# Gaps of 64 bytes between tiles: where moving and stationary operands begin in a partition

## The chip, the cores and the metric

The kernel runs on one core of a Trainium2 chip. The metric is the device time of one execution in microseconds (us). TensorE (PE in the profile) multiplies, VectorE (DVE), ScalarE (ACT) and GpSimd (POOL) do elementwise work, SyncE (SP) issues most of the DMA transfers. On-chip memory (SBUF) has 128 partitions; a tile takes the same range of bytes in each of them.

## What is computed

Two transformer blocks in a row on 256 tokens of width 1024, all in float32. The first block: convolution mixers, attention to a memory of 256 rows, and a PEER layer, which scores all 16,384 experts densely here. The second: two kinds of attention and an MLP. Cut to the parts that fill the time:

```python
def conv_mixers(h, w_in, ...):
    proj = jnp.einsum('bsd,dc->bsc', h, w_in)              # 1024 -> 7168
    ...                                                    
def peer_ffn(h, w_pq, subkeys, u, v):
    q = jnp.einsum('bsd,dq->bsq', h, w_pq)
    ... # 16 best of 128 x 128 experts per token and head: indices and gates
    act = gelu(einsum('chkd,cd->chk', u[idx], h)) * gates
    return einsum('chk,chkd->cd', act, v[idx])             # 16384 experts of width 1024
def second_block(x, ...):
    ...
    y = jnp.square(jax.nn.relu(h2 @ w_up)) @ w_down        # 1024 -> 4096 -> 1024
```

## The kernel before, in words

**Units.** Every weight matrix is cut into units of 128 output columns by 1024 rows (512 KB); there are 493 of them. SyncE loads a unit into a tile `w` (L332), ScalarE rounds it to a high part `wh` (L298), GpSimd, or VectorE in some stages, subtracts that to get a low part `wl` (L302). Each of `w`, `wh`, `wl` has three buffers of 4096 bytes per partition. The activations are kept as a high and a low part too. A product is then high x high, high weight x low activation and low weight x high activation: 24 matmuls of 128 x 128 by 128 x 256 per unit, the 16 with `wh` first, then the 8 with `wl`. Each matmul has its own weight load, and the profile shows the load of the next one under the matmul that runs.

**Stationary and moving.** In `blk` (L380) and `acc_unit` (L1421, L1423, L1425) the unit is stationary and an activation tile moves. In `go_v` (L815 to L819) it is the other way round: `memHL` is stationary and the unit moves. The moving tiles, in the order of the program: `e0a`/`e0b` (L380, first units), `hN` (most of the input projection), `memHL`, `eA`/`eB`, `mg`, `q`, `oA`/`oB`, `p`, then `hA`/`hB` for the 128 units of the experts' first matrix, `zz` for the 128 units of their second, the `s` tiles (second block), `oaHL`/`obHL`, `m`, `eu0`/`eu1` for the 32 units of w_up and `uHL` for the 32 of w_down.

**Stages around the experts.** During units 0 to 47 of the first matrix VectorE finds the best 16 keys and candidates. Then it builds the gates in batches of 8 tokens (L1294, L1298, L1301), which TensorE turns into gate matrices with small matmuls (L1313) that are put between units; the gates of the second group of experts are made during units 48 to 75 and just behind them, those of the first group during units 76 to 127 and the beginning of the second matrix. In the second matrix VectorE also makes the low part of `zz` (L248), one per unit, two units ahead.

**Order.** A planner (`Sched`) with a cost for each operation sets the order when the program is built; each engine then runs its instructions in that order.

**Where tiles lie.** Pools are opened one behind the other, and tiles follow each other in the order of their first use in a pool, each rounded up to 32 bytes. Stages that follow each other take over the same space.

Of the kernel before, what the change touches and what calls it, by code (L numbers as in the profile page):

```python
# [19 lines left out]
F32 = mybir.dt.float32  # L20
# [163 lines left out]
def c_dve(n, ap=0, fast=False):  # L184
    return 66 + n / (1.92 if fast else 0.96) + 60 * ap
# [15 lines left out]
def c_pool(n):  # L201
    return 150 + 2.1 * n
# [8 lines left out]
def tile_kernel(ctx, tc, A, out):  # L211
# [4 lines left out]

    cpool = ctx.enter_context(tc.tile_pool(name="const", bufs=1))
    wpool = ctx.enter_context(tc.tile_pool(name="w", bufs=3))
    epool = ctx.enter_context(tc.tile_pool(name="e", bufs=1))
    mm = ctx.enter_context(tc.tile_pool(name="mm", bufs=4, space=PSUM))  # L220
    ms = ctx.enter_context(tc.tile_pool(name="ms", bufs=4, space=PSUM))
# [28 lines left out]
    def act(o, a, f, **kw):  # L250
        return lambda e="act": ACT.activation(o, a, f, **kw)  # L251

    def either(n):
        return (("dve", c_dve(n), 0.0), ("pool", c_pool(n), 0.0))

    vec = cpool.tile([128, NV], F32, name="vec")
    cst = cpool.tile([128, NCONST], F32, name="cst")
    epsc = cpool.tile([128, 2], F32, name="epsc")
# [4 lines left out]
    def vcol(name, j=0, w=1):  # L263
        return vec[:, VC[name] + j:VC[name] + j + w]
# [170 lines left out]
    def tokens(o, accs, first=True):  # L435

        for t in range(2):
            for i, a in enumerate(accs):
                PE.matmul(o[:, t:t + 1], a[:, t * 128:(t + 1) * 128], onesD[:, 0:1],
                          start=first and t == 0 and i == 0, stop=i == len(accs) - 1, skip_group_check=True)  # L440

    def spread(R, st, bank, ev, n=2, dg=None, copy=()):

        if dg is None:
            dg = cpool.tile([128, n, 128], F32, tag="dg", bufs=1, name="dg")

        def f():
            b = bank()
            for i in range(n):
                PE.matmul(b[:, i * 128:(i + 1) * 128], onesD, dg[:, i], start=i == 0, stop=True, skip_group_check=True)  # L450

        yield Op("dve", 80.0, lambda: V.reciprocal(st, st))
        yield Op("dve", c_dve(n * 128), lambda: V.tensor_tensor(
            dg, ident[:, None, :].to_broadcast([128, n, 128]), st[:, :, None].to_broadcast([128, n, 128]), op=OP.mult))
        yield Op("pe", 215.0 * n, f, ev=(ev, "p"))
        if copy is not None:
            yield Op("act", c_act(n * 128), lambda: ACT.activation(R, bank()[:, :n * 128], AF.Copy), deps=copy, ev=ev)
# [40 lines left out]
    P1 = p1.enter_context(tc.tile_pool(name="p1", bufs=1))  # L498
# [102 lines left out]


    glu = P1.tile([128, 8, 30 + S], F32, name="glu")
    cc = P1.tile([128, 8, S], F32, name="cc")
    POOL.memset(glu[:, :, 0:30], 0.0)
    cfa = {}
# [172 lines left out]
        yield Op("dve", c_dve(S), tt(cfHL[:, 1, j], cc[:, j], cfHL[:, 0, j].bitcast(F32), OP.subtract), ev=("cf", j))  # L779


    kHL = P1.tile([128, 2, 8, S], FR, name="kHL")
    vHL = P1.tile([128, 2, 2, D], FR, name="vHL")

# [737 lines left out]
    P3 = p3.enter_context(tc.tile_pool(name="p3", bufs=1))  # L1522
# [6 lines left out]
    aS2 = P3.tile([128, 2, S], F32, tag="CQ", name="aS2")  # L1529
    RRA = P3.tile([128, 2 * S], F32, name="RRA")  # L1530
    RR, RA = RRA[:, 0:S], RRA[:, S:2 * S]

    def x1_tile(n):
        yield Op("dve", c_dve(S), tt(x1[:, n], xr[:, n], vacc[n // 2][:, (n % 2) * S:(n % 2 + 1) * S], OP.add),
                 ev=("x1", n))
        yield from hl_gain(e02[0][:, n], e02[1][:, n], x1[:, n], g12[:, n:n + 1], S, None, ("xi", n))
# [14 lines left out]

    def x1_stats():
        b = vacc[0][:, 256:260]
        st = P3.tile([128, 4], F32, name="st4")

        def f():
            tokens(b[:, 0:2], [aS1[:, 0], aS1[:, 1]])
            tokens(b[:, 2:4], [aS2[:, 0], aS2[:, 1]], first=False)

        yield Op("pe", 1000.0, f, deps=[("aS", 0, 3), ("aS", 1, 3)])  # L1560

        yield Op("dve", 130.0, lambda: V.tensor_scalar(st[:, 2:4], b[:, 0:2], EPS, None, op0=OP.add))
        yield Op("dve", 130.0, lambda: V.scalar_tensor_tensor(
            st[:, 0:2], st[:, 2:4], EPS, b[:, 2:4], op0=OP.mult, op1=OP.add))
        yield Op("act", 190.0, act(st, st, AF.Sqrt, scale=1.0 / D ** 2))
        dg = T3.tile([128, 2, S], F32, tag="sg", bufs=3, name="sg").rearrange("p a (b t) -> p (a b) t", b=2)
        yield from spread(RRA, st, lambda: vacc[1], "RR", n=4, dg=dg)
        for n in range(8):
            yield Op("dve", c_dve(S, 1), lambda n=n: V.scalar_tensor_tensor(
                xn[:, n], x1[:, n], vcol("final_g", n), RA, op0=OP.mult, op1=OP.mult), ev=("xn", n))  # L1570

    sch.spawn(x1_squares(0), prio=200.0, ready=sch.vt["pe"])
    sch.spawn(x1_squares(1), prio=200.0, ready=sch.vt["pe"])
    sch.spawn(x1_stats(), prio=0.0, ready=sch.vt["pe"])
    acc_last(u_V[128 - NLAST:], vacc, [zs(n) for n in range(128 - NLAST, 128)],
             [("zz", n) for n in range(128 - NLAST, 128)],
# [4 lines left out]
    P3a = p3a.enter_context(tc.tile_pool(name="p3a", bufs=1))  # L1581
# [13 lines left out]
    ckHL = cqk[:, 4:6]  # L1595
    krM = P3a.tile([128, 2, 4, S], FR, name="krM")
    kaM = P3a.tile([128, 2, 2, S], FR, name="kaM")
    vaP = P3a.tile([128, 2, 2, 128], FR, name="vaP")
    vbP = P3a.tile([128, 2, 2, 512], FR, name="vbP")
    qaHL = P3a.tile([128, 2, 4, S], FR, name="qaHL")  # L1600
    qnHL = P3a.tile([128, 2, 4, S], FR, name="qnHL")
    qrHL = P3a.tile([128, 2, 2, S], FR, name="qrHL")
    accq = T3.tile([128, S], F32, tag="acc2", bufs=1, name="accq")
    RQK = P3.tile([128, 2, S], F32, tag="Rq", name="RQK")
    Rq, Rk = RQK[:, 0], RQK[:, 1]
# [585 lines left out]
```

## Time and profile before

| | us |
|---|---|
| median of 3 runs | 1763.25 |
| lowest and highest | 1757.76 and 1767.33 |
| profiled execution, its own time | 1760.9 |
| its span, first to last instruction | 1759.1 |

| engine | busy us | share | instructions |
|---|---|---|---|
| PE | 1587.0 | 90% | 12948 |
| DVE | 1336.5 | 76% | 2197 |
| POOL | 1140.9 | 65% | 486 |
| ACT | 848.8 | 48% | 1463 |

Mean granted TensorE clock: 0.949 of full speed (2.4 GHz); at the lower level it is 0.5 (1.2 GHz).

Matmuls are pipelined: each is shown with some 0.28 us, and the next begins long before it ends. The time of a stream of matmuls is therefore read from their starts. A row of the view in order of time that stands for the 8 matmuls with `wl` comes once per unit, so the distance of two such starts is the time of 24 matmuls. The chain of waits follows the execution back from its last instruction to whatever released each step; its shares say on which engine and line the end depended in a stretch.

### The profile page before, as it was taken

The page shows a single profiled execution, that of the slowest core. Times are in us where ns is not written, and L with a number is a line of the kernel's source. Part 1 is how long each engine was busy: PE and PEld are TensorE (multiplying, and loading weights), DVE is VectorE, ACT ScalarE, POOL GpSimd, SP SyncE. Part 2 cuts the span into 40 slices and gives each one's busy share as a digit, 9 for nine tenths or more (in the row PEclk, how much of TensorE's full clock was granted, in tenths as well). Part 3 has the DMA queues.
Part 4 walks back from the last instruction along what each step waited for, and adds up shares of the span by engine and source line. Part 5 has one row for each costly group of instructions (what it writes and reads, how often), then busy time and mean ns, then how long its engine had stood idle before and what let it go on. Part 6 is the DMA issues. An engine that isn't in the chain of part 4 may idle for free.

```text
span 1759.1 us, 32653 instructions
## 1 busy us (share of the span) xinstructions
PE 1587.0 (90%) x12948; PEld 1562.7 (89%) x12948; DVE 1336.5 (76%) x2197; ACT 848.8 (48%) x1463; POOL 1140.9 (65%) x486
## 2 busy tenths in 40 slices
PE   8899989899999598388997889999999889979997
PEld 7899989889999598278897889999999779979997
DVE  7889967659895778998888998898987896464302
ACT  5544455554445344244444344445455465556533
POOL 6788756456788401057675668888887534758885
PEclk8999989999999799589998999999999899989999
DMA  5565545344555354034443445555555322535553
GB/s 194 169 199 196 168 144 168 120 148 148 165 182 177 103 173 145 1 120 138 139 145 120 143 133 181 187 187 180 182 186 172 121 83 78 179 121 187 181 186 113
DMA packets 75305, 266.69 MB, mean 152 GB/s; under 512 B 8721, under 2 KB 9233, under 8 KB 75153
## 3 DMA queue, kind: packets, MB, share of 16 engines
q1 hardware_dynamic: 73856, 262.77, 45.8%
q8 instruction: 101, 1.65, 0.4%
q10 hardware_dynamic: 1296, 1.85, 0.3%
q14 instruction: 52, 0.42, 0.1%
HBM read 262.48 MB, written 2.10 MB: 150 GB/s over the span
## 4 chain that ended last, share of the span: by engine, by line
PE 65%; DVE 27%; issue 3%; ACT 3%; DMA 1%; POOL 1%; SPq 0%; DVEq 0%; ACTq 0%; POOLq 0%
PE mmb L380 35%; PE msb L1423 8%; PE msb L1425 8%; PE msb L1421 8%; DVE msb L620 3%; DVE ohF L1301 3%; DVE ohF L1298 3%; DVE zz L248 1%; DVE ohF L1294 1%; DVE selT L1301 1%; ACT wh L298 1%; DVE Ah L1333 1%; DVE wl L302 1%; PE msb L1313 1%; DVE prT L1740 1%
## 5 line engine op out<-in xcount | busy, mean ns | idle before, releaser
L302 POOL TENSOR_TENSOR wl<-w,wh 128x1024 fp32r<-128x1024 f32 x451 | 1117.6, 2482 | 588.7 <-ACT wh L298 514.8
L298 ACT ACTIVATE wh<-w 128x1024 fp32r<-128x1024 f32 x491 | 519.1, 1059 | 544.5 <-PE mmb L380 202.2
L248 DVE TENSOR_TENSOR zz<-Ah,zz 128x256 fp32r<-128x256 f32 x128 | 256.9, 2010 | 37.3 <-ACT zz L251 35.8
L380 PE MATMUL mmb<-hA,wh 128*128 128x256 f32 x1024 | 258.4, 289 | 0.0
L380 PE MATMUL mmb<-hB,wh 128*128 128x256 f32 x1024 | 257.0, 287 | 0.0
L1423 PE MATMUL msb<-zz,wh 128*128 128x256 f32 x1008 | 251.1, 286 | 3.5 <-DVE zz L248 3.5
L1421 PE MATMUL msb<-zz,wh 128*128 128x256 f32 x1008 | 251.1, 286 | 0.8 <-DVE Ah L1333 0.8
L380 PEld LDWEIGHTS mmb<-hB,wh 128*128 128x128 f32 x1024 | 201.1, 196 | 0.0
L380 PEld LDWEIGHTS mmb<-hA,wh 128*128 128x128 f32 x1024 | 200.9, 196 | 0.0
L1423 PEld LDWEIGHTS msb<-zz,wh 128*128 128x128 f32 x1008 | 193.9, 192 | 3.7 <-DVE zz L248 3.7
L1421 PEld LDWEIGHTS msb<-zz,wh 128*128 128x128 f32 x1008 | 194.0, 192 | 0.9 <-ACT zz L251 0.9
L380 PE MATMUL mmb<-hA,wl 128*128 128x256 f32 x1024 | 147.4, 287 | 0.0
L1425 PE MATMUL msb<-zz,wl 128*128 128x256 f32 x1008 | 144.3, 286 | 0.0
L380 PEld LDWEIGHTS mmb<-hA,wl 128*128 128x128 f32 x1024 | 134.8, 196 | 0.0
L1425 PEld LDWEIGHTS msb<-zz,wl 128*128 128x128 f32 x1008 | 131.3, 192 | 0.0
L380 PE MATMUL mmb<-hN,wh 128*128 128x256 f32 x896 | 116.3, 281 | 5.5 <-ACT hN L251 5.5
L620 DVE SCALAR_TENSOR_TENSOR msb<-glu,vec,msb 128x256 f32<-128x256 f32 x232 | 113.2, 488 | 6.4
L1313 PEld LDWEIGHTS <-ohF 128*128 128x128 f16 x512 | 41.7, 154 | 85.3 <-DVE selT L1301 42.8
L380 PEld LDWEIGHTS mmb<-hN,wh 128*128 128x128 f32 x896 | 110.3, 192 | 6.0 <-ACT hN L251 5.9
L302 DVE TENSOR_TENSOR wl<-w,wh 128x1024 fp32r<-128x1024 f32 x40 | 63.9, 1599 | 33.2 <-ACT wh L298 31.4
L380 PE MATMUL mmb<-eu,wh 128*128 128x256 f32 x512 | 72.9, 292 | 5.6 <-DVE uHL L484 2.6
L1298 DVE TENSOR_TENSOR ohF<-ohF,selT 128x416 f16<-128x416 f16 (+1 forms) x64 | 77.7, 1214 | 0.3
(487 smaller groups left out, 3256.0 us busy)
## 6 DMA issues: line engine op xcount, KB each, us to landing
w<-in_peer_u_dram SPq DMA_DIRECT2D x128, 512.0 KB, 3.3
w<-in_peer_v_dram SPq DMA_DIRECT2D x128, 512.0 KB, 3.3
w<-in_w_in_dram SPq DMA_DIRECT2D x81, 512.0 KB, 3.3
w<-in_w_up_dram SPq DMA_DIRECT2D x32, 512.0 KB, 3.4
w<-in_w_down_dram SPq DMA_DIRECT2D x32, 512.0 KB, 3.4
w<-in_w_peer_q_dram SPq DMA_DIRECT2D x16, 512.0 KB, 3.6
w<-in_w_v_dram SPq DMA_DIRECT2D x8, 512.0 KB, 3.5
w<-in_sc_w_out_dram SPq DMA_DIRECT2D x8, 512.0 KB, 3.3
```

What stands on the lines that cost most here:

```text
L248: return lambda e="dve": ENG[e].tensor_tensor(o, a, b, op=op)
L298: yield Op("act", c_act(1024), lambda: ACT.activation(h, w, AF.Copy), deps=u["wdep"], ev=("H", u["i"]))
L302: lambda e: ENG[e].tensor_tensor(l, w, h.bitcast(F32), op=OP.subtract), ev=("L", u["i"]))
L380: PE.matmul(p[:, :S], a, b, start=first and n == 0, stop=last and n == len(todo) - 1)
L620: lambda k=k: V.scalar_tensor_tensor(cc[:, j] if k == 30 else o(), glu[:, j, k:k + S], vcol("cf_w", j * 31 + k), o(), op0=OP.mult, op1=OP. ...
L1294: yield Op("dve", 1000.0, lambda: V.tensor_tensor(ohJ, iotax, sel["j"][:, None, sl].to_broadcast([128, 128, 8]), op=OP.is_equal), deps=[(" ...
L1298: yield Op("dve", 400.0 + 8 * NI, lambda: V.tensor_tensor(ohI, iotan()[:, None, i0:i0 + NI].to_broadcast([128, 8, NI]), sel["i"][:, sl][:, ...
L1301: yield Op("dve", 500.0 + 16 * NI, lambda: V.tensor_tensor(gT, ohI[:, :, None].to_broadcast([128, 8, 2, NI]), sel["g"][:, :, sl].rearrange ...
L1313: PE.matmul(banks[c][:, t * 2 * NI:(t + 1) * 2 * NI], ohJ[:, :, ts + t], gT[:, ts + t], start=True, stop=True, skip_group_check=True)
L1421: PE.matmul(o, u["H"][:, d, :], opH, start=first and d % 2 == 0, stop=False, skip_group_check=True)
L1423: PE.matmul(o, u["H"][:, d, :], opL, start=False, stop=False, skip_group_check=True)
L1425: PE.matmul(o, u["L"][:, d, :], opH, start=False, stop=last, skip_group_check=True)
```

## The change

Five calls of a new helper take 64 bytes each and never use them: before the pool of the `e` tiles, before `cc`, before `kHL`, before `vaP`, and behind `qrHL`. The small tile `st4`, 32 bytes after rounding, is written with 128, so that what follows it in its pool moves by 96 more. No instruction is added, removed or moved: the instructions of every engine, with the semaphores that they wait for, stand in the same order; the line numbers and the places of tiles differ.

```diff
+    opool = ctx.enter_context(tc.tile_pool(name="o", bufs=1))
     epool = ctx.enter_context(tc.tile_pool(name="e", bufs=1))
...
+    def shift(pool, name):
+        pool.tile([128, 16], F32, name=name)
+
+    shift(opool, "off")
...
     glu = P1.tile([128, 8, 30 + S], F32, name="glu")
+    shift(P1, "offg")
     cc = P1.tile([128, 8, S], F32, name="cc")
...
+    shift(P1, "offk")
     kHL = P1.tile([128, 2, 8, S], FR, name="kHL")
     vHL = P1.tile([128, 2, 2, D], FR, name="vHL")
...
     RR, RA = RRA[:, 0:S], RRA[:, S:2 * S]
+    st4 = P3.tile([128, 32], F32, name="st4")
...
-        st = P3.tile([128, 4], F32, name="st4")
+        st = st4[:, 0:4]
...
     kaM = P3a.tile([128, 2, 2, S], FR, name="kaM")
+    shift(P3a, "offv")
     vaP = P3a.tile([128, 2, 2, 128], FR, name="vaP")
...
     qrHL = P3a.tile([128, 2, 2, S], FR, name="qrHL")
+    shift(P3a, "offq")
```

The tiles that matter begin here (byte within a partition, and the remainder by 128; tiles under one tag begin at the same byte):

| tiles | before | remainder | after | remainder |
|---|---|---|---|---|
| `w`, `wh`, `wl` (three each, 4096 apart) | 28128 to 60896 | 96 | the same | 96 |
| tags `e0a`, `e0b`, `e1a`, `e1b`: `e0`, `q`, `p`, `s`, `m`; `eA`/`eB`, `mg`, `oA`/`oB`, `hA`/`hB`, `zz`, `eu` | 64992 to 89568 | 96 | 65056 to 89632 | 32 |
| `memHL` | 122336 | 96 | 122400 | 32 |
| `hN`, `qHL` | 156064 | 32 | 156192 | 32 |
| `kHL`, `vHL` | 172448, 188832 | 32 | 172640, 189024 | 96 |
| `pTs` of the first block | 138720 | 96 | 138784 | 32 |
| `uHL`, `obHL`, `cqk`; `oaHL` | 142848; 202240 | 0 | 143008; 202528 | 32 |
| `krM`, `kaM`; `pTs` of the second block | 151040, 159232; 210432 | 0 | 151200, 159392; 210720 | 32 |
| `vaP`, `vbP`, `qaHL`, `qnHL`, `qrHL` | 163328 to 189952 | 0 | 163552 to 190176 | 96 |

Slices of these tiles that one matmul reads begin at multiples of 512 bytes within them, so the difference between moving and stationary, taken by 128, is that of the tiles. Counted over the matmuls with split (float32r) operands of the built program: before, 9,794 have a difference of 0, 1,392 of 64, 1,090 of 32 or 96; after, 12,162 have 64 and 114 have 0.

## Rows read from the trace of the kernel before

**Rows 1.** The page's chain that ended last: shares of the span by engine

```profile
PE 65%; DVE 27%; issue 3%; ACT 3%; DMA 1%; POOL 1%; SPq 0%; DVEq 0%; ACTq 0%; POOLq 0%
```

**Rows 2.** In order of time, TensorE: start us, length us, instruction, merged count

```profile
97.71 1.12 PE L819 MATMUL mmb<-wl,memHL 128*128 128x256 f32 x8
100.59 1.12 PE L819 MATMUL mmb<-wl,memHL 128*128 128x256 f32 x8
...
120.34 1.07 PE L380 MATMUL mmb<-hN,wl 128*128 128x256 f32 x8
123.06 1.07 PE L380 MATMUL mmb<-hN,wl 128*128 128x256 f32 x8
...
357.91 1.52 PE L1038 MATMUL msb<-pTs,vHL 128*128 128x256 f32 x12
...
1200.97 1.12 PE L1425 MATMUL msb<-zz,wl 128*128 128x256 f32 x8
1203.85 1.12 PE L1425 MATMUL msb<-zz,wl 128*128 128x256 f32 x8
...
1700.70 1.10 PE L1425 MATMUL msb<-uHL,wl 128*128 128x256 f32 x8
1703.53 1.10 PE L1425 MATMUL msb<-uHL,wl 128*128 128x256 f32 x8
```

**Rows 3.** Chain of waits by line, stretches 227:448, 448:587, 607:700 and 1052:1352

```profile
by line: PE mmb L380 44.6%; DVE hT L248 5.4%; issue 3.9%; ACT wh L298 3.8%; DVE acc L248 2.8%; DMA w<-in_w_peer_q_dram 2.8%; PE msb L1038 2.7%; PE msb L1147 2.7%; PE msb L999 2.3%; DVE wl L302 2.2%; DVE accp L248 1.9%; DVE prs L1016 1.9%; A
by line: PE mmb L380 99.5%; ACT Ah L1259 0.3%; ACT selT L1214 0.2%; PE msb L1147 0.1%; issue 0.0%
by line: PE mmb L380 89.4%; PE msb L1313 6.4%; DVE Ah L1328 1.0%; DVE ohF L1301 1.0%; PE msb L1210 0.7%; DVE ohF L1294 0.6%; DVE ohF L1298 0.5%; ACT hT L1325 0.4%; issue 0.3%; ACT Ah L1259 0.0%
by line: PE msb L1425 32.7%; PE msb L1421 32.6%; PE msb L1423 32.6%; PE msb L1486 1.0%; DVE se0b L489 0.6%; DVE x L248 0.4%; PE mmb L1313 0.2%; issue 0.0%
```

**Rows 4.** The same, stretches 758:948, 948:1052, 1352:1502 and 1502:1751

```profile
by line: PE mmb L380 36.8%; DVE ohF L1301 18.9%; DVE ohF L1298 17.1%; DVE Ah L1264 5.0%; DVE Ah L1333 4.8%; issue 4.6%; DVE msb L1331 4.6%; DVE ohF L1294 3.8%; PE msb L1313 2.7%; ACT accp L1325 1.6%; ACT mmb L1263 0.2%; DVE selT L1301 0.1%
by line: DVE zz L248 22.5%; issue 17.1%; DVE selT L1301 11.6%; PE msb L1423 8.8%; PE msb L1421 8.5%; PE msb L1425 8.3%; DVE Ah L1333 6.5%; DVE mmb L1331 5.5%; DVE ohF L1294 3.4%; PE mmb L1313 3.1%; DVE ohF L1298 1.6%; ACT hT L1325 1.1%; ACT
by line: PE mmb L380 16.8%; DVE prT L1740 8.2%; DVE aS L248 5.7%; DVE xn L1569 4.5%; issue 4.1%; PE msb L1809 3.7%; DVE mmb L248 3.6%; PE msb L380 3.4%; DVE mxT L1729 3.1%; DVE prT L1757 2.8%; DVE mxT L1731 2.8%; DVE prT L1768 2.5%; DMA w<-
by line: PE mmb L380 42.6%; PE msb L1421 11.4%; PE msb L1425 11.4%; PE msb L1423 11.3%; PE mmb L1961 3.1%; PE mmb L1959 3.0%; PE mmb L1960 3.0%; PE msb L1486 2.3%; DVE xn L248 1.8%; DVE eu L489 1.6%; ACT wh L298 1.3%; DVE yg L248 1.1%; DVE 
```

**Rows 5.** By stretch: busy (count) of PE, PEld, DVE, ACT, POOL; clock, DMA

```profile
607.00:700.00 93.00, 90.06 (x770) 89.26 (x768) 68.84 (x91) 45.77 (x85) 7.17 (x3) 0.98 0.49 159
700.00:758.00 58.00, 23.09 (x184) 19.14 (x185) 56.20 (x101) 15.72 (x42) 2.82 (x1) 0.50 0.00 1
758.00:948.00 190.00, 169.19 (x1394) 164.80 (x1393) 165.09 (x233) 85.31 (x166) 133.16 (x51) 0.97 0.45 145
948.00:1052.00 104.00, 84.09 (x660) 81.98 (x661) 100.61 (x123) 42.37 (x82) 64.82 (x25) 0.92 0.41 132
1052.00:1352.00 300.00, 300.00 (x2505) 299.96 (x2504) 258.94 (x163) 146.66 (x219) 249.48 (x104) 1.00 0.56 182
```

**Rows 6.** Pieces of the chain, 824:850: start us, length us, what

```profile
828.60 2.78 DVE ohF L1298
...
831.72 3.31 DVE ohF L1301
...
836.63 9.21 PE mmb L380 x64
```

**Rows 7.** Pieces of the chain, 790:870

```profile
818.90 7.71 PE mmb L380 x64
```

**Rows 8.** In order of time, second matrix of the experts: idle before in brackets

```profile
1199.48 2.39 POOL L302 TENSOR_TENSOR wl<-w,wh 128x1024 fp32r<-128x1024 f32 x1 [0.49 <-ACT wh L298]
1199.74 2.41 DVE L248 TENSOR_TENSOR zz<-Ah,zz 128x256 fp32r<-128x256 f32 x1 [0.27 <-ACT zz L251]
1201.22 1.06 ACT L298 ACTIVATE wh<-w 128x1024 fp32r<-128x1024 f32 x1 [1.51 <-PE msb L1423]
1202.36 2.40 POOL L302 TENSOR_TENSOR wl<-w,wh 128x1024 fp32r<-128x1024 f32 x1 [0.49 <-ACT wh L298]
```

**Rows 9.** The same view, input projection, GpSimd alone

```profile
121.73 2.40 POOL L302 TENSOR_TENSOR wl<-w,wh 128x1024 fp32r<-128x1024 f32 x1 [0.32 <-ACT wh L298]
124.45 2.41 POOL L302 TENSOR_TENSOR wl<-w,wh 128x1024 fp32r<-128x1024 f32 x1 [0.32 <-ACT wh L298]
```

## The prediction

> **What bounds the kernel now.** I first read the chain of waits as a whole: TensorE carries 65% of the span, VectorE 27% [rows 1]. The kernel waits for matmuls most of the time, but not in every stage. Since the change moves no instruction and only places tiles elsewhere, I then looked for anything in the trace that depends on place, and the spacing of the matmuls does. It is read from starts [rows 2], each pair 24 matmuls apart:
> - `memHL` with `wl`: 100.59 - 97.71 = 2.88 us, 120.0 ns per matmul; `zz` with `wl`: 1203.85 - 1200.97 = 2.88 us, 120.0 ns. Both have a difference of 0.
> - `hN` with `wl`: 123.06 - 120.34 = 2.72 us, 113.3 ns, at a difference of 64.
> - `uHL` with `wl`: 1703.53 - 1700.70 = 2.83 us, 117.9 ns, at a difference of 32.
>
> The shape, the type and the instruction are the same in all of them. `memHL` and `hN` stand 20 us apart in one stage, with the same weight buffers and the same work beside them. One more row has a difference of 64: `pTs` moving over `vHL`, 12 matmuls in 1.52 us [rows 2]. With a last one of 0.28 us that leaves 1.24 us for 11 steps, 113 ns. There the moving operand lies 64 above the stationary one, with `hN` 64 below, so the sign does not matter. After the change the large tiles have the remainders of `hN` before, 32 against 96. I therefore take 113.3 ns for all of them.
>
> **The change part by part.** *The gaps* cost nothing: no instruction uses them. Transfers and elementwise work have no row of their own at another place; the tiles of one stage at remainders 96, 32 and 0 are written and read by the same operations without a visible order among them, so I set their change to 0, and let plus or minus 3 us stand for it in the range.
>
> *The matmuls.* From a difference of 0, one matmul gains 120.0 - 113.3 = 6.7 ns, or 5.6%; from 32, 117.9 - 113.3 = 4.6 ns, or 3.9%. All 9,794 and 1,090 together would be 65 + 5 = 70 us; at the low clock nothing is gained, since a matmul at half the clock takes longer than either (an assumption that only lowers the sum). That is an upper bound. What reaches the end is the part that lies on the chain, so I take each stretch's share of TensorE in the chain:
>
> - Before 227: the six `memHL` units in the projection, 144 x 6.7 ns = 1.0 us. `hN` is at 64 already and gains nothing.
> - 227 to 448: 44.6% of 221 us [rows 3] is 98.6 us; 192 matmuls on `hN`'s tile (`cf`) take 22 of it; 76.6 x 5.6% = 4.3, and 4.1 with short low-clock stretches taken off.
> - 448 to 587, experts 0 to 47: 99.5% of 139 us [rows 3], 138.3 x 5.6% = 7.7.
> - 607 to 700: 89.4% of 93 us [rows 3], 83.1 x 5.6% = 4.6, less a start at low clock, 4.3.
> - 587 to 607 and 700 to 758: 0. In the second, TensorE is busy 23 of 58 us, VectorE 56 [rows 5]; a faster TensorE only waits longer.
> - 758 to 948, gates beside experts 76 to 127: 36.8% of 190 us [rows 4], 69.9 x 5.6% = 3.9, less the matmuls of slow rounds, 3.2. A round, 836.63 - 818.90 = 17.7 us [rows 6, 7], has 64 matmuls on the chain; 64 others run under VectorE's part and gain nothing.
> - 948 to 1052: 25.6% of 104 us [rows 4] is 26.6; up to 1.5, and some of it at the low clock (0.92 granted, rows 5): 1.0.
> - 1052 to 1352, second matrix: 98.9% of 300 us [rows 3], 296.7 x 5.6% = 16.5.
> - 1352 to 1502, attention: L380 16.8% of 150 us [rows 4], 25.2 x 5.6% = 1.4.
> - 1502 to 1751: L380 42.6% of 249 us [rows 4], 106 x 5.6% = 5.9, less low clock 5.6; `uHL` 36.4%, 90.6 x 3.9% = 3.5; `oaHL`/`obHL` 9.1%, 22.7 x 3.9% = 0.9.
>
> The sum is 1.0 + 4.1 + 7.7 + 4.3 + 3.2 + 1.0 + 16.5 + 1.4 + 5.6 + 3.5 + 0.9 = 49 us.
>
> *What is late next.* In the second matrix the supply of weights has to come every 2.72 us instead of 2.88. The input projection shows that this can be: there GpSimd starts a `wl` every 124.45 - 121.73 = 2.72 us and still idles 0.32 [rows 9]. In 758 to 948 TensorE gets through its units earlier while VectorE's part of the round stays, so it idles more, and the granted clock may fall more often. A round with such a fall is on record: the same 64 matmuls take 9.21 us instead of 7.71 [rows 6, 7]. I charge two more of these, 3 us; the bounds are 0 and 8 rounds, 12 us.
>
> So 1760.9 - 49 + 3 = 1715 us, from the profiled execution's own time, which lies 2.35 us below the median of the runs (1763.25) and within their spread of 9.6.
>
> *A rule that speaks against this.* The Trainium skill, "TensorE: Matmul & The Clock Gate", section "Step-by-step: what each phase is for", says that TensorE has two independent read ports on SBUF, one for the moving operand and one for weight loads, so that loading the next weights takes no bandwidth from the running matmul. By that rule the place of one against the other could not matter, the matmul term would be 0 and the time would stay at 1761. The trace does not agree with it: 120.0 and 113.3 ns in one stage [rows 2].
>
> **The rivals.**
> - *GpSimd and VectorE take turns in the second matrix.* There VectorE's `zz` takes 2.41 us, from 1199.74 to 1202.15, and ends 0.28 after GpSimd's `wl`, which runs from 1199.48 to 1201.87; GpSimd starts again at 1202.36 [rows 8]. If 0.49 us between two `wl` is what this turn needs, 2.39 + 0.49 = 2.88 is its own period, and TensorE's 2.88 hides it. Then the 16.5 us are not gained: 1731. For it: the numbers meet. Against it: the profile puts the 0.49 down to ScalarE's `wh`, VectorE is done 0.21 before GpSimd starts, and ScalarE itself waits 1.51 us for TensorE to release the buffer [rows 8]. The need is 2.39 + 0.28 = 2.67, under 2.72, but by 0.05 only. The Trainium skill, "SBUF — State Buffer", section "Who interferes with whom", says that a VectorE instruction with two SBUF inputs contends with a GpSimd instruction that reads SBUF; the rows agree, a subtraction of 256 elements in 2.41 us.
> - *More comes back than the chain shows.* VectorE's long steps in the gate rounds, 2.78 and 3.31 us [rows 6], stand behind GpSimd's `wl`, which follows TensorE's release of a buffer; if all of that moves up too, the sum goes towards the bound, 70 less some 4 at the low clock: 1695.
> - *The change does not do what it says*, because the spacing follows something else than the difference by 128, for instance the stage or the tile's length: 1761. Against it: two signs, two stages and the `memHL`/`hN` pair.
> - *Slower: the clock in 758 to 948.* From 700 to 758 TensorE is busy 40% and gets 0.50 of its clock [rows 5]. If the gate rounds fell to that level for good, 52 x 24 = 1,248 matmuls would cost up to 113 ns more each, 141 us, of which TensorE's idle time there, 190 - 169 = 21 us [rows 5], absorbs a part: 1715 + 120 = 1835. It makes the kernel slower once more than about half of these matmuls run low. Against it: TensorE is busy 89% there with 0.97 granted, would be about 86% busy, and 948 to 1052 still gets 0.92 at 81% [rows 5].
>
> **How the numbers follow.** The forecast, 1715 within some 10 us, has 0.75. Turns of GpSimd and VectorE (1731): 0.11. More than the chain (1695): 0.07. No effect (1761): 0.04. The clock (1835): 0.03. A measurement of this kernel tells about 0.5%, 9 us, from no change; the first three cases are faster by more, 0.93; same 0.04; slower 0.03. The range reaches from 1700, most of the way to the third case, to 1735, which takes in the second with 4 us of the runs' spread; what is left out is about 0.15.
>
> **What would show it.** In the changed kernel's profile a `zz` or `hA` row with `wl` should come every 2.72 us, `uHL` too, and the stretch of the second matrix should shrink from 300 to some 283 us with TensorE busy throughout. GpSimd's idle before `wl` should fall from 0.49 to about 0.3 there, and the stretch in which VectorE alone finishes the second group's gates, 58 us with TensorE busy 23 [rows 5], should get no shorter. The forecast is wrong if the spacing stays at 2.88 (the difference is not the cause), if the spacing is 2.72 but GpSimd becomes the releaser of TensorE in the second matrix, or if the granted clock falls well under 0.949 in the mean.

## The result, and the profile after

| | before | after |
|---|---|---|
| median, us | 1765.29 (4 runs, 1757.76 to 1767.45) | 1744.34 (4 runs, 1739.88 to 1746.74) |
| profiled execution, us | 1760.9 | 1739.88 |
| its span, us | 1759.1 | 1738.1 |

The ratio is 0.9886, 95% interval 0.9848 to 0.9924: 13 to 27 us faster, 21 by the medians and 21.0 between the two profiled executions. The direction of the forecast came true, its size did not: 1744 instead of 1715, outside the range.

The page's chain, answering to [rows 1], has lost only two points of TensorE:

```profile
PE 63%; DVE 29%; issue 3%; ACT 2%; DMA 1%; POOL 1%; SPq 0%; DVEq 0%; ACTq 0%; POOLq 0%
```

The rows that answer to [rows 2] are again TensorE's in order of time (start us, length us, instruction, merged count); two rows of one operand lie 24 matmuls apart. After:

```profile
99.33 1.10 PE L827 MATMUL mmb<-wl,memHL 128*128 128x256 f32 x8
102.16 1.10 PE L827 MATMUL mmb<-wl,memHL 128*128 128x256 f32 x8
...
121.95 1.10 PE L386 MATMUL mmb<-hN,wl 128*128 128x256 f32 x8
124.78 1.10 PE L386 MATMUL mmb<-hN,wl 128*128 128x256 f32 x8
...
1199.28 1.10 PE L1433 MATMUL msb<-zz,wl 128*128 128x256 f32 x8
1202.11 1.10 PE L1433 MATMUL msb<-zz,wl 128*128 128x256 f32 x8
...
1691.76 1.07 PE L1433 MATMUL msb<-uHL,wl 128*128 128x256 f32 x8
1694.48 1.07 PE L1433 MATMUL msb<-uHL,wl 128*128 128x256 f32 x8
```

`zz` comes every 2.83 us, 117.9 ns per matmul: not 113.3 as forecast, but 2 ns under the 120.0 of before. `hN` ran at 113.3 and now also takes 2.83. Only `uHL` reached the forecast: 2.72 us, 113.3 ns. So place matters, but not by the rule that the prediction took from the rows. Counted by 256 bytes and with the sign, moving minus stationary, the operands went from 0 to +64 (e tiles, `zz`), from -64 to +64 (`hN`), from +32 to -64 (`uHL`) and, with `memHL` stationary, from 0 to -64.

By stage (first number the stretch, then its length, busy time and count of PE, PEld, DVE, ACT, POOL, then clock and DMA) the trace of before reads, for experts 0 to 47, for the gates with what runs beside them, and for the second matrix:

```profile
447.90:585.40 137.50, 137.50 (x1148) 137.50 (x1148) 111.36 (x359) 67.83 (x99) 120.44 (x47) 1.00 0.54 173
585.40:1060.00 474.60, 376.65 (x3089) 364.86 (x3088) 416.99 (x572) 195.21 (x388) 218.93 (x84) 0.89 0.38 124
1060.00:1351.90 291.90, 291.90 (x2434) 291.90 (x2434) 250.85 (x157) 143.63 (x215) 242.49 (x102) 1.00 0.56 183
```

The same work in the trace after:

```profile
442.20:577.10 134.90, 134.90 (x1147) 134.90 (x1147) 113.68 (x358) 68.18 (x100) 119.72 (x47) 1.00 0.52 177
577.10:1049.60 472.50, 370.85 (x3089) 358.54 (x3088) 417.99 (x573) 194.83 (x387) 225.70 (x84) 0.88 0.36 124
1049.60:1336.10 286.50, 286.50 (x2434) 286.50 (x2434) 254.08 (x156) 143.11 (x214) 247.63 (x102) 1.00 0.55 187
```

Where TensorE is busy without a gap, the stretch shrinks by 1.9%, 2.6 and 5.4 us, much as 2.2 of 120 ns per matmul make (1.8%). The middle stretch, with VectorE busy 418 us of 472, hardly moves.

### The profile page after: what moved, and what is told of

The parts are those of the page before. It is cut to its first block, busy times and chain, and to the rows that moved or that the text cites. A ratio compares the mean times of both kernels' runs of the same rounds, so it can differ in the third digit from the quotient of the medians.

```text
span 1738.1 us, 32653 instructions
## 1 busy us (share of the span) xinstructions
PE 1564.5 (90%) x12948; PEld 1538.9 (89%) x12948; DVE 1340.6 (77%) x2197; ACT 849.3 (49%) x1463; POOL 1154.0 (66%) x486
## 4 chain that ended last, share of the span: by engine, by line
PE 63%; DVE 29%; issue 3%; ACT 2%; DMA 1%; POOL 1%; SPq 0%; DVEq 0%; ACTq 0%; POOLq 0%
PE mmb L386 34%; PE msb L1433 8%; PE msb L1431 8%; PE msb L1429 8%; DVE msb L627 3%; DVE ohF L1306 3%; DVE ohF L1309 3%; DVE zz L249 1%; DVE selT L1309 1%; DVE ohF L1302 1%; DVE scr L1208 1%; DVE hT L249 1%; DVE Ah L1341 1%; DVE scr L1205 1%; ACT wh L304 1%
## 5 line engine op out<-in xcount | busy, mean ns | idle before, releaser
L308 POOL TENSOR_TENSOR wl<-w,wh 128x1024 fp32r<-128x1024 f32 x451 | 1130.7, 2511 | 554.6 <-ACT wh L304 482.9
L386 PE MATMUL mmb<-hA,wh 128*128 128x256 f32 x1024 | 251.5, 284 | 0.0
L1431 PE MATMUL msb<-zz,wh 128*128 128x256 f32 x1008 | 247.7, 283 | 3.5 <-DVE zz L249 3.5
L386 PE MATMUL mmb<-hB,wh 128*128 128x256 f32 x1024 | 249.9, 282 | 0.0
L1429 PE MATMUL msb<-zz,wh 128*128 128x256 f32 x1008 | 247.8, 283 | 0.8 <-DVE Ah L1341 0.8
L386 PEld LDWEIGHTS mmb<-hA,wh 128*128 128x128 f32 x1024 | 195.5, 191 | 0.0
L386 PEld LDWEIGHTS mmb<-hB,wh 128*128 128x128 f32 x1024 | 195.4, 191 | 0.0
```

The source lines that it names most:

```text
L308: lambda e: ENG[e].tensor_tensor(l, w, h.bitcast(F32), op=OP.subtract), ev=("L", u["i"]))
L386: PE.matmul(p[:, :S], a, b, start=first and n == 0, stop=last and n == len(todo) - 1)
L1429: PE.matmul(o, u["H"][:, d, :], opH, start=first and d % 2 == 0, stop=False, skip_group_check=True)
L1431: PE.matmul(o, u["H"][:, d, :], opL, start=False, stop=False, skip_group_check=True)
```

## The experiments

Four theories for the spacing stood at the start. A: 113 ns comes only where both operands begin in one half of 256 bytes, 64 apart. B: the signed difference by 256 decides. C: the difference by 128 alone, the prediction's own. D: not place. Later came E to J, named in the expectations. "-64" is moving minus stationary by 256. Tables of streams are worked out from starts of back-to-back matmuls at the full clock; a spacing quoted from rows of a whole kernel is a difference of two starts over 24. Each cut of a diff is against the changed kernel, unless something else is said.

**All pairs in steps of 32 bytes.** No computation, only 16 stationary and 16 moving tiles:

```diff
+    for i in range(16):
+        for j in range(16):
...
+            for r in range(24):
+                PE.matmul(b[:, :S], st[i][:, 0:128], mv[j][:, 0:S], start=r == 0, stop=r == 23)
```

> Leaves out the whole computation. 16 stationary tiles sA to sP begin at 0, 32, ... 480 bytes past a multiple of 512, 16 moving tiles mA to mP likewise; each of the 256 pairs runs 24 matmuls of the kernel's shape back to back, nothing else runs. Read from starts: 24 x 120.0 = 2.88 us, 24 x 117.8 = 2.83, 24 x 113.3 = 2.72 per pair. Theory A (halves): 2.72 us only where both begin in the same 128-byte half of 256 bytes and 64 apart in it; 2.83 where they lie in different halves; 2.88 where they begin at the same place by 256. For sP (480, where the kernel's weights lie) this gives 2.72 with mF (160) and mN (416), 2.83 with mB (32), 2.88 with mP (480); for sB (32) 2.72 with mD (96), 2.83 with mH (224). Theory B (sign): 2.72 us where the moving operand begins 64 below the stationary one by 256, 2.83 at 64 above: sP as in A, but sB 2.72 with mH (224) and 2.83 with mD (96). Theory C (as I predicted, difference by 128 alone): 2.72 for sP with mB, mF, mJ less 64 and all others 64 apart by 128. Theory D (not the place, but the supply of weights or other engines' reads): the same spacing in all 256 pairs.

Measured, moving minus stationary and mean ns: 0: 119.8; +32: 117.7; +64: 117.7; +96: 119.6; 128: 118.6; -96: 117.4; **-64: 113.3**; -32: 118.3. Every diagonal of the 16 by 16 table has one value within some 1 ns, with 6 exceptions, all at -64, where 117.7 came instead; the -64 above is that of the other 26. Rows for the stationary tile at 192, with moving tiles at 128, 192, 256 and 384 (24 matmuls each):

```profile
299.18 2.99 PE L240 MATMUL bankA<-mE,sG 128*128 128x256 f32 x24
...
304.84 3.04 PE L240 MATMUL bankA<-mG,sG 128*128 128x256 f32 x24
...
310.55 2.99 PE L240 MATMUL bankA<-mI,sG 128*128 128x256 f32 x24
...
321.92 2.89 PE L240 MATMUL bankA<-mM,sG 128*128 128x256 f32 x24
```

The first and the last are both at -64: 2.99 us is the slow value, 2.89 the fast one. A, C and D fall; B fits, but for the six. The table agrees with before and after: 0 is 120, +64 and +32 are 118, -64 is 113. But it says too that -64 has two values.

**Everything at -64.** All four moving operands of the units 160 by 256, `wh` and `wl` 224:

```diff
-    shift(opool, "off")
+    shift(opool, "off", 48)
...
-    st4 = P3.tile([128, 32], F32, name="st4")
+    st4 = P3.tile([128, 4], F32, name="st4")
...
-    shift(P3a, "offv")
...
-    shift(P3a, "offq")
...
+    shift(P3b, "offu", 56)
```

> The changed kernel with the gap ahead of the e tiles 192 bytes instead of 64, st4 as before, a gap of 224 bytes ahead of uHL and no gaps in the attention of the second block, so that e tiles, hN, memHL and uHL begin at 160 by 256 and the weights at 224. Theories A and B: 113.3 ns in hN, hA/hB, zz, eu and uHL; of the chain's 49 us (my prediction's sum, without oaHL) some 45 to 48 are gained, and the time is 1714 to 1720 where before is 1764. memHL stationary at 160 under moving weights at 224: A 113.3, B 117.8. Theory C: as the changed kernel, 1744. Rival on GpSimd and VectorE: zz keeps 2.80 us or more per unit and the second matrix of the experts stays over 292 us, the time over 1728.

Measured: 1725.99 us (6 runs, 1723.9 to 1743.83), ratio 0.9829 [0.9786, 0.9873]: a gain, but short of the 1714 to 1720 of A and B. In its trace `hA` and `hB` ran at 113.3 for the first 48 units, but `zz`, `eu` and `uHL` at 118, at the same difference:

```profile
501.80 1.07 PE L386 MATMUL mmb<-hA,wl 128*128 128x256 f32 x8
504.52 1.07 PE L386 MATMUL mmb<-hA,wl 128*128 128x256 f32 x8
...
1196.66 1.11 PE L1433 MATMUL msb<-zz,wl 128*128 128x256 f32 x8
1199.49 1.11 PE L1433 MATMUL msb<-zz,wl 128*128 128x256 f32 x8
```

**The same program again.**

> The kernel with everything at 160 once more. Theory E (at -64 each restart of a stream takes one of two spacings): the same program shows its stretches of 113 and 118 ns in other places than in its first trace, the times scatter, 1715 to 1745, and the mean ratio stays 0.975 to 0.99. If the places and the order of instructions alone fix the spacing, the stretches are where they were: hA at 113, zz, eu and uHL at 118.

Measured: 1726.02 us (6 runs, 1719.81 to 1732.31), ratio 0.9800 [0.9766, 0.9834]. Now `hA` is slow, 2.82 us, and `zz` fast, 2.72:

```profile
502.13 1.11 PE L386 MATMUL mmb<-hA,wl 128*128 128x256 f32 x8
504.95 1.11 PE L386 MATMUL mmb<-hA,wl 128*128 128x256 f32 x8
...
1136.15 1.07 PE L1433 MATMUL msb<-zz,wl 128*128 128x256 f32 x8
1138.87 1.07 PE L1433 MATMUL msb<-zz,wl 128*128 128x256 f32 x8
```

Instructions, order and places are identical, so something that differs from one execution to the next chooses between the two spacings. (The two executions were on two chips as well, which the record does not separate.)

**Only `hN` put back.** The change with `hN` at -64 as before:

```diff
-    shift(P1, "offg")
+    shift(P1, "offg", 48)
```

> The changed kernel with the gap ahead of cc 192 bytes instead of 64, so that hN alone goes back to 160 by 256, where it lay before; all else of the large tiles as in the changed kernel. Theories A and B: hN 113.3 ns again, e tiles stay at 117.8. If the projection's matmuls are on the path, 95 us of the chain get 3.8% shorter, 3.6 us under the changed kernel, 1741; if VectorE's convolution takes up the difference, no change, 1744. Theory C: hN stays at 117.8, 1744.

Measured: 1743.73 us (6 runs, 1741.54 to 1744.2), ratio 0.9911 [0.9881, 0.9941], which overlaps the change's 0.9848 to 0.9924. `hN` ran at 113.3 for most of the projection and was through at 198 us instead of 202, but the stage behind it began no earlier, at 226.9 us against 226.1; the chain there belongs to VectorE's convolution, the first entry of the chain by line from 100 to 226 us in that run:

```profile
by line: DVE msb L627 40.8%; PE mmb L386 35.1%; PE mmb L827 3.7%; PE mmb L823 3.6%; PE mmb L825 3.6%; DVE wl L308 3.1%; issue 3.0%; DVE gs L249 1.7%; DVE cc L627 1.5%; DVE msb L623 1.3%; DVE msb L739 1.0%; PE msb L746 0.6%; DVE mmb L249 0.3
```

So `hN`'s loss shows no cost in the time. The e tiles did not stay at 117.8, as A and B expected: at +64, `hA` and `hB` ran at 113.3 here through all of the first 48 units.

```profile
500.36 1.07 PE L386 MATMUL mmb<-hA,wl 128*128 128x256 f32 x8
503.08 1.07 PE L386 MATMUL mmb<-hA,wl 128*128 128x256 f32 x8
```

The run also caught a switch. `zz`, at +64 as in the change, ran at 113.3 from 1053 us on, until TensorE once had to wait for VectorE, and at 118 from there to the stage's end:

```profile
1180.99 1.07 PE L1433 MATMUL msb<-zz,wl 128*128 128x256 f32 x8
1183.71 1.07 PE L1433 MATMUL msb<-zz,wl 128*128 128x256 f32 x8
1185.22 0.39 PE L1431 MATMUL msb<-zz,wh 128*128 128x256 f32 x1 [0.32 <-DVE zz L249]
...
1192.81 1.10 PE L1433 MATMUL msb<-zz,wl 128*128 128x256 f32 x8
1195.64 1.10 PE L1433 MATMUL msb<-zz,wl 128*128 128x256 f32 x8
```

**Steps of 16 bytes, entered in nine ways.** No computation; a stationary tile at 0, a moving operand that begins 0 to 240 bytes further:

```diff
+    for d in range(0, 256, 16):
+        for k in (16, 48, 80, 112, 144, 176):
+            V.tensor_copy(scr[:, 0:k], bank[0][:, 0:k])
+            stream(0, d, 40)
+        stream(1, 0, 24)
+        stream(0, d, 40)
+        stream(1, 192, 40)
+        stream(0, d, 40)
+        stream(1, 64, 40)
+        stream(0, d, 40)
```

> The kernel leaves the whole computation out. One stationary tile of 128 columns, one moving tile of 256 columns that begins 0, 16, 32, ... 240 bytes further on by 256. For each of the 16 differences: six streams of 40 matmuls, each behind a break of another length (VectorE copies 16 to 176 columns out of the bank first), and then three streams of 40 without a break before them: behind 24 matmuls at difference 0, behind 40 at 192 (-64) and behind 40 at 64. Theory E (at a difference of -64 and of +64 there are two steady spacings, 113.3 and 117.7 ns, and how the stream began decides which; at 0 there is one, 119.8): at 192, and perhaps at 64, the six restarts and the three entries fall apart into 113 and 118, each keeping its value to its end; at 0 all are 119.8. Theory F (the place alone decides, and the mixture in the kernels comes from weights or other engines' work around it): all nine streams of a difference agree within 0.5 ns; at 192 all are 113.3, at 64 all 117.7. A finer step than 32 may show a difference at which 113 ns is held whatever came before; theory E has no number for that, theory F expects the 16-byte places to lie between their neighbours, 113 to 120.

Measured, last 24 steps of each stream: at 0 all nine 120.0; at 96 all nine 120.0; at 192 (-64) six at 113.3 and three at 117.8; at 64 one at 113.3 and eight at 117.8; at 112 all nine at 113.3. Not every other place is steady either: +16 gave 113.3 to 120.0. The same pair restarted, at 192, the first three of the six:

```profile
717.42 4.98 PE L234 MATMUL bankA<-mov,sta 128*128 128x256 f32 x40 [0.27 <-DVE scr L239]
722.70 4.82 PE L234 MATMUL bankA<-mov,sta 128*128 128x256 f32 x40 [0.30 <-DVE scr L239]
727.86 4.83 PE L234 MATMUL bankA<-mov,sta 128*128 128x256 f32 x40 [0.33 <-DVE scr L239]
```

F falls and E holds: the spacing at a given place can depend on how the stream began. And 112 showed a place that seemed to need no luck.

**A difference of 112 by shifting the weights.** `wh` and `wl` become slices of one tile, 16 bytes further on, at 240; the moving operands lie at 96 (against the kernel with everything at -64):

```diff
-    shift(opool, "off", 48)
+    shift(opool, "off", 24)
...
+    whl = wpool.tile([128, 6 * 1024 + 8], FR, bufs=1, name="whl")
+
+    def part(n):
+        return whl[:, 4 + 1024 * n:4 + 1024 * (n + 1)].rearrange("p (k c) -> p k c", k=8)
...
-        h = wpool.tile([128, 8, 128], FR, tag="wh", bufs=NH, name="wh")
+        h = part(u["i"] % 3)
```

> The six buffers of wh and wl are slices of one tile whl that begins 16 bytes further on, at 240 by 256; e tiles, hN, memHL and uHL begin at 96, a difference of 112 from whl. The instructions stand in the order of before. Theory E (at a difference of 112 one spacing, 113.3 ns, is reached from every start): hA, zz, eu, uHL and hN run at 113.3 ns in every long stretch. If the rest of the prediction's sum is right, its 49 us come back: 1712 to 1718; counted from the kernel with all at 160, whose second matrix and w_down ran at 118, 11 and 7 us less, 1708. Rival G (faster matmuls don't reach the end, since VectorE and GpSimd set the pace of the second matrix at about 2.8 us per unit): spacing 113.3 but breaks between units, 1724 to 1730. Rival F (place alone doesn't decide): stretches at 118 remain, 1720 to 1745.

Measured: 1761.93 us (12 runs, 1749.27 to 1766.82), ratio 0.9993 [0.9971, 1.0016], and 2.88 us, 120.0 ns:

```profile
1195.17 1.12 PE L1438 MATMUL msb<-zz,whl 128*128 128x256 f32 x8
1198.05 1.12 PE L1438 MATMUL msb<-zz,whl 128*128 128x256 f32 x8
```

A miss of all three theories; F's 118 did not come in the long stretches either. The control has the one tile without the shift, in the kernel before:

> Control for the tile whl alone: the same six slices of one tile, with every matmul operand at the remainders of before (difference 0 for the e tiles). Theory E: 120.0 ns as in before, ratio 0.995 to 1.005. Should the one tile itself save time, the ratio falls below 0.99 and the 112 run has to be read against this one.

Measured: 1759.52 us (10 runs, 1750.56 to 1763.75), ratio 0.9983 [0.9958, 1.0008]: the tile itself costs or saves nothing beyond noise.

**Both operands in steps of 16 bytes.** No computation, 256 pairs, two streams of 24 each behind a break:

```diff
+    for s in range(0, 256, 16):
+        for m in range(0, 256, 16):
+            for k in (16, 64):
+                V.tensor_copy(scr[:, 0:k], bank[0][:, 0:k])
+                stream(0, s, m, 24)
```

> The kernel leaves the whole computation out. Stationary and moving operand begin at 0, 16, ... 240 by 256 each, 256 pairs, two streams of 24 matmuls per pair, each behind a break. The question is why 240 against 96 (112 apart) ran at 120.0 ns in the whole kernel, where 0 against 112 ran at 113.3. Theory H (the stationary operand's own place counts: a weight load that begins 16 bytes off a multiple of 32 reads one line more, and a difference of 112 helps only a load that is on a multiple): rows of stationary places that are odd multiples of 16 hold no 113, 118 to 120 throughout, and a row at a multiple of 32 repeats the row at 0. Theory I (only the difference counts, and the kernel's 120 comes from the other engines' traffic): each diagonal has one value, 113.3 at 112 in all 16 rows. Theory J (the two start spacings can be had at any place, so the table is a draw of lots): values at one difference scatter by more than 1 ns between rows without regard to odd or even, and the two streams of a pair disagree in over a quarter of the pairs.

Measured: at a difference of 112 all 16 streams whose stationary operand begins at a multiple of 32 run at 113.3, and of the 16 others 14 at 120.0 and 2 at 117. Rows for 0 against 112 and for 16 against 128:

```profile
63.46 3.02 PE L234 MATMUL bankA<-mov,sta 128*128 128x256 f32 x24 [0.27 <-DVE scr L241]
66.80 3.02 PE L234 MATMUL bankA<-mov,sta 128*128 128x256 f32 x24 [0.32 <-DVE scr L241]
...
178.48 3.15 PE L234 MATMUL bankA<-mov,sta 128*128 128x256 f32 x24 [0.27 <-DVE scr L241]
181.94 3.14 PE L234 MATMUL bankA<-mov,sta 128*128 128x256 f32 x24 [0.32 <-DVE scr L241]
```

I falls. H holds on this diagonal and gives the 120.0 of the run before, but its wider claim falls: rows at odd multiples of 16 do hold 113.3, in all 16 of their streams at -64 (at multiples of 32 it is 15 of 16) and in 8 of 16 at +64. No run shows the extra line that H supposes. J falls as a draw of lots: odd and even places differ, the two streams of a pair are more than 1 ns apart in 35 of 256 pairs and not in a quarter, and the 8 pairs at +64 that disagree all do it alike, with 113.3 behind the shorter break and 118.3 behind the longer. Whether the break or the order does that is not tested. One more place is fast at times: +16 gave 113.3 in 7 of the 16 streams at multiples of 32.

**A difference of 112 by shifting the moving operands.** `wh` and `wl` stay at 224, a multiple of 32; the `e1` tiles (`hA`, `hB`, `zz`, `eu`, and others) and `uHL` begin at 80:

```diff
+    def etile(shape, dt, tag, name):
+        if tag[:2] == "e0":
+            return epool.tile(shape, dt, tag=tag, name=name)
+        t = epool.tile([128, 2056], dt, tag=tag, name=name)[:, 4:2052]
...
-    uHL = P3b.tile([128, 2, 32, S], FR, name="uHL")
+    uHL = P3b.tile([128, 64 * S + 8], FR, name="uHL")[:, 4:4 + 64 * S].rearrange("p (a k t) -> p a k t", a=2, k=32)
```

> wh and wl stay at 224 by 256, a multiple of 32; the tiles eA, mg, oA, hA, hB, zz and eu begin at 80 (slices that start 16 bytes into their tile), and so does uHL: a difference of 112 from a stationary place that is a multiple of 32. The e0 tiles lie at 32 (difference 64), hN and memHL at 160 (-64). Theory H (there 113.3 ns is reached from every start): hA and hB, zz, eu and uHL run at 113.3 ns in every long stretch of the trace; the second matrix is then held up by VectorE's zz and angS and gives back some 10 us and not 16.5, so 1712 to 1722, ratio 0.972 to 0.980, with less scatter than at -64. Theory J (each stretch draws one of the two spacings here too): stretches of 118 or 120 ns remain, 1722 to 1745, ratio 0.980 to 0.992. If slices that start 16 bytes into a tile slow ScalarE or VectorE, their durations rise (zz 2.4 us, wh 1.06 us) and the time with them.

Measured: 1723.83 us (5 runs, 1722.22 to 1728.03), ratio 0.9815 [0.9792, 0.9838], just outside H's 1712 to 1722 and inside J's range; the spacings are those of H. Every long stretch of those operands runs at 113.3, and ScalarE's `wh` did not get slower (1.06 us). The runs lie within 6 us of each other, against 12 and 20 at -64, but the kernel with only `hN` put back did so within 3, so this scatter tells little:

```profile
500.48 1.07 PE L395 MATMUL mmb<-hA,wl 128*128 128x256 f32 x8
503.19 1.07 PE L395 MATMUL mmb<-hA,wl 128*128 128x256 f32 x8
...
1136.25 1.07 PE L1445 MATMUL msb<-zz,wl 128*128 128x256 f32 x8
1138.97 1.07 PE L1445 MATMUL msb<-zz,wl 128*128 128x256 f32 x8
...
1689.85 1.07 PE L1445 MATMUL msb<-uHL,wl 128*128 128x256 f32 x8
1692.57 1.07 PE L1445 MATMUL msb<-uHL,wl 128*128 128x256 f32 x8
```

Its stages, to be read against the two tables above (the first and the last stretch hold 9 and 7 matmuls fewer than those of before, worth 1.0 and 0.8 us):

```profile
441.40:570.30 128.90, 128.90 (x1139) 128.90 (x1139) 116.85 (x358) 66.32 (x97) 118.92 (x46) 1.00 0.57 183
570.30:1047.50 477.20, 371.80 (x3105) 359.02 (x3104) 425.69 (x574) 196.87 (x392) 231.95 (x85) 0.87 0.38 124
1047.50:1325.60 278.10, 276.48 (x2427) 275.43 (x2426) 258.88 (x156) 142.18 (x211) 250.58 (x102) 1.00 0.59 192
```

**The changed kernel again**, beside the second run at -64 on one chip:

> The changed kernel once more beside the others: ratio 0.985 to 0.992, and by theory E mostly 117.8 ns (at +64 one stream in nine of the fine run took 113), with other stretches at 113 than in its first trace, if any.

Measured: 1746.89 us (6 runs, 1739.98 to 1753.81), ratio 0.9905 [0.9873, 0.9937]; all its long streams of e tiles at 118. But `uHL`, which took 2.72 us in the first trace of the same program, takes 2.82 in this one:

```profile
1689.90 1.10 PE L1433 MATMUL msb<-uHL,wl 128*128 128x256 f32 x8
1692.72 1.11 PE L1433 MATMUL msb<-uHL,wl 128*128 128x256 f32 x8
```

The version at -64 was 21 us faster beside it, and it and the kernel at 112 beat both kernels of this change.

## Why the prediction was wrong

The mechanism was right in part: place changes the spacing, no instruction moves, and the time falls. What it left out is that one place can have two spacings. The step that failed is "the sign does not matter ... I therefore take 113.3 ns for all of them". It rested on 12 matmuls of `pTs` at +64 [rows 2] and made one rule of two signs. The grid gives +64 as 117.7, and the large tiles measured 117.9 after the change. The 113 of `pTs` was no error: a stream at +64 can run at either spacing. The trace of before held two warnings that I did not look for. The group of `pTs` 18 us earlier takes 1.57 us for the same 12 matmuls, some 117 ns each by the same working. And `hN`, the prediction's own example of 113.3, takes 2.83 us there as well, with the same buffers, 140 us later:

```profile
339.89 1.57 PE L1038 MATMUL msb<-pTs,vHL 128*128 128x256 f32 x12
...
265.56 1.10 PE L380 MATMUL mmb<-hN,wl 128*128 128x256 f32 x8
268.39 1.10 PE L380 MATMUL mmb<-hN,wl 128*128 128x256 f32 x8
```

A rule by place alone could not have given both, and the price should have had 117.9 as its other bound. That `uHL` came out as forecast, 3.4 us of the gain, was luck: in the second execution of the same program it ran at 117.8.

The last shift of the moving operands tests the rest of the sum, since there the price is the one that the prediction used (its `e0` tiles stayed at 118, and so did `hN` in most of its stretches). TensorE runs the same 12,948 instructions in the same order in all these traces, so the table goes from one instruction to the same one in the other trace. Gains in us against the profiled execution of before:

| stretch | predicted | after (118 ns) | after, second execution | 112 apart (113.3 ns) |
|---|---|---|---|---|
| start to first unit of the experts | 5.1 | 5.7 | -0.9 | 6.5 |
| experts 0 to 47 | 7.7 | 2.6 | 2.6 | 7.0 |
| gates and experts 48 on, to the second matrix alone | 8.5 - 3 | 2.1 | 0.3 | -0.1 |
| second matrix | 16.5 | 5.4 | 5.4 | 12.8 |
| attention | 1.4 | 0.3 | -1.2 | 1.0 |
| from there to the end | 10.0 | 4.9 | 1.8 | 9.9 |
| sum | 46 | 21.0 | 7.9 | 37.1 |

- *The chain's share times the saving per matmul* came out where TensorE has no gaps: 7.7 against 7.0, 16.5 against 12.8 (with 1.6 us of waits for VectorE in it), 10.0 against 9.9. With 2.2 ns in place of 6.7 the terms of the e tiles (49 - 3.5 - 0.9 = 44.6) give 15, and `uHL` its 3.5 in full: 18, inside the interval of 13 to 27. The two executions of the change, 21.0 and 7.9, lie on either side of that, so the 21.0 is not to be read as a sum that came true.
- *The gates.* Of the terms 4.3, 3.2 and 1.0 the first, 607 to 700 us, came out: 4.0 at 112 apart, 2.3 after. The second measured 1.0 and 3.2, the third -5.0 and -3.0. But in the third, 948 to 1052 us, the execution of before is the quick one: the control with the one tile, whose operands begin where they did, takes 3.3 us longer there. Over the whole stretch the executions with changed spacings gain between -1.7 and 9.4 us (the second at -64 has the 9.4), so no price is shown for it. VectorE is busy 417 to 426 us of 472 to 477 in the three kernels of the tables above, and the clock falls from 0.89 to 0.88 and 0.87. VectorE itself got slower there: its 64 instructions `ohF<-selT` (L1294) take 49.9 us before, 50.8 after, 55.6 in both executions at -64 and 60.4 at 112 apart, and 50.0 in the kernel with shifted weights, which ran at 120 ns. What slows them is not tested. The 3 us for the clock went in the right direction.
- *The first stretch* gained 5.7 at 118 ns, where 2 were due, by luck. TensorE was 4.6 us behind at the end of the projection, through `hN`, and level again at 226 us (0.4 us ahead). From 304 to 344 us it gained 3.2, at a granted clock of 0.95 against 0.91 in before. The second execution of the change had 0.92 there and reached the experts 0.9 us later than before.
- *GpSimd and VectorE in turns* (rival, 1731): refuted in size. At 2.72 us per unit TensorE has 276.5 of 278.1 us busy. The waits that there are, 1.6 us in five and the one at 1185 above, come from VectorE being late with `zz`, and at +64 such a wait restarted a stream that then took its other spacing.
- *More than the chain* and *the clock at 1.2 GHz in the gates*: neither happened; the mean clock was 0.950, against 0.949 before. *The change does not do what it says* was near in one respect: the spacing follows something more than the difference by 128.
- *The rule on two independent read ports* (the Trainium skill, "TensorE: Matmul & The Clock Gate", section "Step-by-step: what each phase is for"): the grids contradict what the prediction drew from it, that place could not matter. Shape, type and work are the same in all their streams, only the two operands' places and what ran before differ, and the spacing goes from 113.3 to 120.0 ns. Whether the two reads meet at one port or elsewhere no run shows.

Left open: what chooses between 113.3 and 117.8 at -64 and +64 when a stream starts, and why a start at -64 takes the fast one in 31 of 32 streams of the last grid, in 6 of 9 of the nine ways, and in some stretches only of the kernels. Nor is it shown to be chance, since the last grid's pairs at +64 repeat each other. No run shows the mechanism in the chip behind the table of places.

## What to carry over

When matmuls of one shape come at different spacings in a trace, look up where their operands begin, by 256 bytes and with the sign, and measure all pairs in a kernel that does nothing else before moving anything; a rule from three rows is too short. Look through every stretch of one operand, not at one pair of rows, since a stream can hold one of two spacings until its next break. A saving per matmul reached the end where TensorE has no gaps; in a stretch with VectorE busy 88% of the time it gave -1.7 to 9.4 us from one execution to the next, so put no fixed price on it. And trace a program twice: two executions of this one gained 21.0 and 7.9 us.

## What the runs showed of the hardware that was not expected

- Back-to-back matmuls of 128 x 128 by 128 x 256 in fp32r, each with its own weight load, at the full clock: 113.3 to 120.0 ns, by moving minus stationary start by 256 bytes. With the stationary operand at a multiple of 32 bytes, 0 and +96 are slowest (120), -64 and +112 fastest (113.3, at -64 not always).
- +112 keeps 113.3 from every start tried, but only if the stationary operand begins at a multiple of 32 bytes; 16 bytes off it is 120.0 in 14 of 16 streams and 117 in two.
- At -64 and +64 a stream holds 113.3 or 117.8 ns until it is interrupted: 286 us without a switch at 118, 131 us at 113, with a switch at a wait of 0.32 us. Not every wait switches it: in the second execution at -64 `zz` kept 113.3 through several.
- One program ran the same stage at 2.72 us per unit in one execution and 2.83 in another, on two chips. How much of the scatter between runs this makes is open: the kernel before, whose e tiles hold 120.0, scatters by 14 us too (1753.06 to 1767.38).
